# One diffusion step of a two-layer hybrid mixer: first modulation by three operations from PSUM, four early products of x in place of six, and branch parameters set up where the branches begin

## The chip, the cores and the metric

The kernel runs on one core of a Trainium2 chip. The core has five engines that each work through their own list of instructions in order and wait for each other by semaphores: TensorE (PE, matrix products into the accumulation memory PSUM), VectorE (DVE), ScalarE (ACT), GpSimd (POOL) and SyncE (SP, which here only starts transfers from main memory). The metric is the time of one execution on the device in microseconds, as the median of several runs.

## The reference

384 tokens (128 of context, 256 latent) with 2048 channels go through two layers. Each layer modulates its input, multiplies it with one large matrix, runs four branches (an RG-LRU, a neighbourhood attention, a grouped-query attention, an mLSTM), and multiplies their gated outputs with a second matrix:

```python
mod = jax.nn.silu(cond) @ lp['ada_w'] + lp['ada_b']          # 2048 -> 3 * 2048, one row per token kind
shift, scale, gate = jnp.split(mod, 3, axis=-1)
xm = rmsnorm(x, lp['norm_w']) * (1.0 + scale) + shift
pr = split_projection(xm @ lp['w_in'])                       # 2048 -> 7184
...                                                          # branches A to D on slices of pr
y = jnp.concatenate([out_a, out_b, out_c, out_d], axis=-1) @ lp['w_out']
x = x + gate * y
```

Before the first product with `w_in`, then, the norm of x over all 2048 channels and the first values of `shift` and `scale` have to be there. The branches need small per-channel parameters: the RG-LRU the log sigmoid of `lru_lambda` and half of its gate biases, the mLSTM a quarter of its output norm.

## The kernel before

The tokens lie along the free dimension, the channels in 16 chunks (index k) of 128 partitions. Every product in float32 is made of three products of rounded parts: x is split into `xh` and `xl`, each weight tile into `wh` (a rounded copy, made by ACT from the tile `raw` that SP has fetched) and `wl` (the rest, `raw - wh`, made by POOL in pieces of 256 columns). There are three buffers for `raw`. A weight tile covers two chunks k and up to 512 columns.

Layer 0 makes eight passes over the groups of columns `vif`, `ml_q`, `ml_k`, `ml_o`, `lru_gate`, `ml_v`, `lru_x`, `na_q`, `gqa_k`, each pass with two chunks k, because the modulation of all chunks is not known at once. The modulation itself comes in 12 parts s for each layer: part 0 of layer 0 by 16 matmuls of PE (`ada_pe`, two values of k at a time), all others by DVE (`ada_dve`), which multiplies 16 tiles `araw` of the modulation weights (256 KB each, called slices below) with two scalars each and sums in the tile `sbp`, two `SCALAR_TENSOR_TENSOR` to a slice, and then folds the sum (`STREAM_TRANSPOSE`, `TENSOR_REDUCE`, one matmul and the operations on `picked`, in `ada_final`). Part s of layer 0 gives the shift and scale of chunks 2s and 2s + 1.

The list `START` sets the order of the beginning: fetch x and square it, with the matmuls of part 0 between; token `r` makes the inverse norm `rbc` of each token (`rstd_bc`) and multiplies the first chunks of x with it on DVE (`unit_rms`, the early products). The other chunks are multiplied by POOL, in two halves of 128 and 256 tokens, each asked for by `modulate0` of an earlier chunk. `modulate0` makes `xh` on ACT, straight from the multiplied x, and `xmt` and `xl` on DVE. After the last matmul of part 0, ACT copies the row out of PSUM, PE transposes it in four small pieces into a scratch bank, and DVE makes `mod` (the shift) and `Amul` (norm weight times one plus scale) of chunks 0 and 1.

`setup_params` prepares the parameters of the branches: some 20 operations of DVE on tiles of 8 or 16 columns and one exponential on ACT. A helper `defer` runs a function once a counter of the matmul time written so far has passed a number. The scheduler of the framework then decides the final order on each engine, and SP's list holds the fetches of `raw` and of slices in one queue: a fetch of `raw` that waits for its buffer holds back the slices behind it.

Of the kernel before, what the change touches and what calls it, by code (L numbers as in the profile page):

```python
# [16 lines left out]
KC = D // 128  # L17
# [60 lines left out]
def tile_hybrid_step(ctx: ExitStack, tc: tile.TileContext, I, O):  # L78
# [32 lines left out]
    def defer(dt, fn):  # L111
        deferred.append([clock["now"] + dt, fn])
# [33 lines left out]
    def sm(i, n, name):  # L146
        return wrk.tile([128, n], F32, name=name, tag=f"m{i}", bufs=2)

    pers_all = consts.tile([128, T + 384 + PP_W + DEPTH * 128 + 264], F32, name="pers")
    used = [0]  # L150

    def pers(n):
# [13 lines left out]
    def P(n, l=None, parts=2):  # L166
        a, b = PP[n]
        if l is None:
            return prm[:, a:b]
        s = (b - a) // parts  # L170
        return prm[:, a + l * s:a + (l + 1) * s]
# [24 lines left out]
    def stt(out, a, s, b, op0, op1):  # L196
        return nc.vector.scalar_tensor_tensor(out, a, s, b, op0=op0, op1=op1)  # L197
# [32 lines left out]
    def setup_params():  # L230
# [4 lines left out]
        nc.vector.tensor_scalar(hbi, P("bi"), 0.5, None, op0=OP.mult)  # L235
        nc.vector.tensor_scalar(mln, P("mlnorm"), 0.25, None, op0=OP.mult)


    ada_acc = dict(done=0)
    last_ev = {}  # L240

    def order(later, earlier):
        tc.add_manual_dep(later, earlier.name,
                          mybir.DependencyInfo(mybir.DependencyClass.NoSync, mybir.DependencyReason.DATA),
                          reason="issue order")

    def traced(fn):
        bb = nc.cur_bb.bb
        n = len(bb.instructions)
        fn()  # L250
        return bb.instructions[n:]
# [4 lines left out]
                last_ev["v"] = ins  # L256


    def ada_final_mod(l, j0, nj):
        v = mod[:, l, j0:j0 + nj, :]  # L260
        b = P("ada_b", l)[:, j0:j0 + nj]
        nc.vector.tensor_tensor(v, v, b[:, :, None].to_broadcast([128, nj, 2]), op=OP.add)
        if 16 <= j0 < 32:
            nb = P("norm", l)[:, j0 - 16:j0 - 16 + nj]
            stt(Amul[:, l, j0 - 16:j0 - 16 + nj, :], v, 1.0, nb[:, :, None].to_broadcast([128, nj, 2]),
                OP.add, OP.mult)

    sbp = pada.tile([128, 1024], F32, name="sbp")

    def ada_pe(it):  # L270
        t = it["t"]
        raw = it["raw"]
        if t == 0:
            ada_acc["pe"] = accb[3]
        ps = ada_acc["pe"]
        for kk in range(2):
            k = 2 * t + kk
            nc.tensor.matmul(ps[0:2, :], scond[:, k, :], raw[:, kk, :], start=k == 0, stop=k == KC - 1)
        if it["stop"]:
            row = w(0, "adarow")  # L280
            act(row[0:2, :], ps[0:2, :], AF.Copy)
            pt = scr("adat")
            for q in range(4):
                nc.tensor.transpose(pt[:, 2 * q:2 * q + 2], row[0:2, q * 128:(q + 1) * 128], ident[0:2, 0:2])
            for i, j0 in enumerate((0, 16)):
                nc.vector.tensor_copy(mod[:, 0, j0:j0 + 2, :], pt[:, 4 * i:4 * i + 4].rearrange("p (q c) -> p q c", c=2))
                ada_final_mod(0, j0, 2)
            ada_acc["done"] += 1

    quarter = pers(4)  # L290
# [34 lines left out]
    def ada_dve(it):  # L325
        raw = it["raw"]

        def piece(c):
            it["left"] -= 1
            l, s, k = it["l"], it["s"], it["k"]  # L330
            acc = sbp[:, c * 512:(c + 1) * 512]
            sc = scond[:, k, c:c + 1]
            if it["start"]:
                d = nc.vector.tensor_scalar(acc, raw, sc, None, op0=OP.mult)  # L334
            else:
                d = stt(acc, raw, sc, acc, OP.mult, OP.add)
            if "v" in last_ev:
                order(d.ins, last_ev["v"])

        def fold(c):  # L340
            l, s = it["l"], it["s"]
            acc = sbp[:, c * 512:(c + 1) * 512]
            if c == 0:
                ada_acc["red"] = sm(15, 32, "red")
            red = ada_acc["red"]
            turned = wrk.tile([128, 512], F32, name="turned", tag="adasb", bufs=2)
            d = nc.vector.transpose(turned, acc)
            nc.vector.tensor_reduce(red[:, c * 16:(c + 1) * 16], turned.rearrange("p (g i) -> p g i", i=32),
                                    axis=AX.X, op=OP.add)
            if "v" in last_ev:  # L350
                order(d.ins, last_ev["v"])
            if c == 1:
                finals.append((clock["now"] + FLAG, lambda: ada_final(l, s, red)))

        it["left"] = 2
        for c in range(2):
            backlog.append(lambda c=c: piece(c))
        for c in range(2 if it["stop"] else 0):
            backlog.append(lambda c=c: fold(c))
# [95 lines left out]
    def unit_rms(k, eng):  # L455
        for a in (0, TP) if eng is nc.gpsimd else (0,):
            b = T if a or eng is nc.vector else TP
            eng.tensor_tensor(xr[k][:, a:b], xr[k][:, a:b], rbc[:, a:b], op=OP.mult)

    def modulate0(k):  # L460
        x = xr[k]
        t = wrk.tile([128, T], F32, name="xmt", tag="t15", bufs=4)
        for c, (a, b) in enumerate(SEG):
            act(xh[k][:, a:b], x[:, a:b], AF.Identity, bias=mod[:, 0, k, c:c + 1], scale=Amul[:, 0, k, c:c + 1])
        for c, (a, b) in enumerate(SEG):
            nc.vector.tensor_scalar(t[:, a:b], x[:, a:b], Amul[:, 0, k, c:c + 1], mod[:, 0, k, c:c + 1],
                                    op0=OP.mult, op1=OP.add)
        xl[k] = big.tile([128, T], F32R, name=f"xl{k}", tag=f"xl{k}", bufs=1)
        nc.vector.tensor_sub(xl[k], t, xh[k].bitcast(F32))  # L469
        if 6 <= k + 4 < KC:  # L470
            unit_rms(k + 4, nc.gpsimd)

    def split_cat(k):
        act(xh[k], cat[:, k, :], AF.Copy)
# [1074 lines left out]
    for tok in START:  # L1549
        if tok == "x":  # L1550
            for k in xq[0]:
                nc.sync.dma_start(xr[k], I["xT"][:, k, :])
            for k in xq.pop(0):
                square_in(k, xr[k], nc.vector)
        elif tok == "w":
            upto("w", wl, w_dma, pos["w"] + 1)
        elif tok == "r":
            rstd_bc()
            for k in range(6):
                unit_rms(k, nc.vector)  # L1560
        elif tok == "P":
            it = first.pop(0)
            a_dma(it)
            ada_pe(it)
        elif tok == "D":
            it = a_items[pos["a"]]
            upto("a", a_items, a_dma, pos["a"] + 1)
            ada_dve(it)
            it["early"] = True
# [4 lines left out]
    for it in plan:  # L1574
# [6 lines left out]
        elif ty == "mod":  # L1581
            l = it["l"]
            mods.extend((it["req"], l, k) for k in it["ks"] if (l, k) not in ready)
            if it["first"]:
                upto("w", wl, w_dma, cur_w + 4)
                if l == 0:
                    upto("a", a_items, a_dma, n_first + NADA - 1)
                    load_consts()
                for k in it["ks"]:
                    need(l, k)  # L1590
                if l == 0:
                    defer(60.0, setup_params)
        elif ty == "split":
            whole.clear()
            for n4 in range(2):
# [128 lines left out]
```

## Time and profile before

| what | value |
|---|---|
| runs | 1468.54, 1468.83, 1475.76 us, median 1468.83 us |
| the profiled execution | 1480.24 us, of which the span on the core is 1478.4 us |
| PE busy | 1415.2 us, 96% of the span |
| DVE busy | 1080.4 us, 73% |
| POOL busy | 914.5 us, 62% |
| ACT busy | 828.1 us, 56% |

The profiled execution took 11.4 us more than the median run. PE is busy nearly all of the time, so the page's shares say little on where time can be gained: what counts are the stretches in which PE stands still, and what it waits for there. The page's slices show the granted clock of PE at seven tenths of full speed in the first slice of 37 us and at eight tenths in the second.

### The profile page before, as it was taken

The numbers are of one execution on the slowest core, as the hardware profiler recorded it, in microseconds if no ns is written. First come the engines' busy times: TensorE is split into PE (matmuls) and PEld (weight loads), VectorE is DVE, ScalarE is ACT, GpSimd is POOL, SyncE is SP. The second block draws the span as 40 slices with busy tenths as digits, with TensorE's granted clock in tenths as the row PEclk, the third lists the DMA queues.
The fourth block names the chain that finished last, engine by engine and source line by source line (L and its number), as shares of the span: only waits on it lengthen the run. The fifth ranks groups of instructions, "written<-read, shape, count | busy, mean of one in ns | idle before, by whom it ended". The sixth has DMA issues, their size and how long they took to land. (4 is left out here: it accounts for less than half of the span.)

```text
span 1478.4 us, 23865 instructions
## 1 busy us (share of the span) xinstructions
PE 1415.2 (96%) x7999; PEld 1331.2 (90%) x7999; DVE 1080.4 (73%) x2050; ACT 828.1 (56%) x1638; POOL 914.5 (62%) x1242
## 2 busy tenths in 40 slices
PE   6889999899999999999989999999999999899997
PEld 1879999798998799999989999999999789799997
DVE  4889999998899948858568998447667760943533
ACT  4579999765546776553343434234454877363432
POOL 1856666656566765755737666675656774555762
PEclk7899999999999999999999999999999999899999
DMA  8777878686677555565748877654547344355433
GB/s 271 242 231 250 240 230 253 197 253 180 180 209 239 163 165 161 206 222 195 233 130 263 249 243 231 181 159 122 173 142 232 100 128 133 104 175 171 146 122 96
DMA packets 167519, 281.67 MB, mean 191 GB/s; under 512 B 17380, under 2 KB 49380, under 8 KB 167268
## 3 DMA queue, kind: packets, MB, share of 16 engines
q1 hardware_dynamic: 159520, 272.40, 60.4%
q10 hardware_dynamic: 7876, 7.75, 1.6%
q8 instruction: 62, 1.02, 0.3%
q14 instruction: 61, 0.50, 0.1%
HBM read 271.17 MB, written 8.93 MB: 189 GB/s over the span
## 5 line engine op out<-in xcount | busy, mean ns | idle before, releaser
L1284 POOL TENSOR_TENSOR wl<-raw,wh 128x256 fp32r<-128x256 f32 (+1 forms) x1152 | 864.9, 785 | 477.5 <-ACT wh L193 414.3
L1402 PE MATMUL acc<-xh,wh 128*128 128x384 f32 x1630 | 568.1, 349 | 20.0 <-ACT xh L193 10.0
L1402 PE MATMUL acc<-xl,wh 128*128 128x384 f32 x1630 | 554.2, 340 | 0.0
L1402 PE MATMUL acc<-xh,wl 128*128 128x384 f32 x1630 | 552.2, 339 | 0.2 <-POOL wl L1284 0.2
L197 DVE SCALAR_TENSOR_TENSOR sbp<-araw,pers,sbp 128x512 f32<-128x512 f32 x690 | 517.6, 750 | 27.2 <-DMA araw<-in_ada_n 15.6
L193 ACT ACTIVATE wh<-raw 128x1024 fp32r<-128x1024 f32 (+2 forms) x304 | 307.0, 1013 | 324.9 <-PE acc L1402 248.6
L1402 PEld LDWEIGHTS acc<-xh,wh 128*128 128x128 f32 x1630 | 309.0, 190 | 25.7 <-ACT xh L193 10.4
L1402 PEld LDWEIGHTS acc<-xl,wh 128*128 128x128 f32 x1630 | 308.6, 189 | 1.5
L1402 PEld LDWEIGHTS acc<-xh,wl 128*128 128x128 f32 x1630 | 308.1, 189 | 1.2 <-POOL wl L1284 1.1
L1402 PE MATMUL acc<-wh,xl 128*128 128x512 f32 (+2 forms) x452 | 165.4, 366 | 5.4 <-DVE xl L469 2.7
L1402 PE MATMUL acc<-wl,xh 128*128 128x512 f32 (+2 forms) x452 | 163.9, 363 | 0.0
L1402 PE MATMUL acc<-wh,xh 128*128 128x512 f32 (+2 forms) x452 | 163.0, 361 | 0.0
L1402 PEld LDWEIGHTS acc<-wh,xl 128*128 128x128 f32 x452 | 88.5, 196 | 19.3 <-DVE xl L469 4.6
L1402 PEld LDWEIGHTS acc<-wl,xh 128*128 128x128 f32 x452 | 88.0, 195 | 12.5
L1402 PEld LDWEIGHTS acc<-wh,xh 128*128 128x128 f32 x452 | 88.0, 195 | 12.1
L197 DVE SCALAR_TENSOR_TENSOR cat<-acc,pers,xold 128x128 f32<-128x128 f32 (+1 forms) x56 | 20.3, 409 | 66.7 <-PE acc L1402 66.7
L193 ACT ACTIVATE cat<-acc 128x384 f32<-128x384 f32 (+1 forms) x94 | 46.2, 495 | 5.4 <-PE acc L1402 4.8
L193 ACT ACT_TABLE_LOAD x26 | 33.4, 1283 | 10.2 <-DVE arena L891 7.9
L193 ACT ACTIVATE xh<-cat 128x384 fp32r<-128x384 f32 x32 | 16.5, 519 | 40.0 <-PE acc L1402 24.0
L389 DVE TENSOR_TENSOR arena<-arena,sq 128x384 f32<-128x384 f32 x38 | 25.8, 679 | 16.0 <-ACT sq L193 14.5
L1402 PE MATMUL s<-xh,wh 128*128 128x384 f32 x98 | 34.1, 348 | 1.2 <-ACT cat L193 1.2
L334 DVE TENSOR_SCALAR sbp<-araw,pers 128x512 f32<-128x512 f32 x46 | 34.3, 745 | 0.2
(338 smaller groups left out, 1824.0 us busy)
## 6 DMA issues: line engine op xcount, KB each, us to landing
raw<-in_w_in SPq DMA_DIRECT2D x208, 512.0 KB, 4.0
araw<-in_ada_n SPq DMA_DIRECT2D x368, 256.0 KB, 4.3
raw<-in_w_out SPq DMA_DIRECT2D x64, 512.0 KB, 4.0
raw<-in_w_in SPq DMA_DIRECT2D x32, 256.0 KB, 3.0
araw<-in_ada_n SPq DMA_DIRECT2D x8, 512.0 KB, 5.4
xr<-in_xT SPq DMA_DIRECT2D x16, 192.0 KB, 5.7
nac<-in_nac SPq DMA_DIRECT2D x8, 288.0 KB, 4.3
xold<-in_xT SPq DMA_DIRECT2D x3, 768.0 KB, 6.4
```

The costliest lines, as they stand in the source:

```text
L193: return nc.scalar.activation(out, in_, f, bias=bias, scale=scale)
L197: return nc.vector.scalar_tensor_tensor(out, a, s, b, op0=op0, op1=op1)
L334: d = nc.vector.tensor_scalar(acc, raw, sc, None, op0=OP.mult)
L389: eng.tensor_tensor(sqacc, sqacc, s, op=OP.add)
L1284: nc.gpsimd.tensor_tensor(it["lo"][:, kk, cs], raw[:, kk, cs], hv[:, kk, cs], op=OP.subtract)
L1402: last_ev["pe"] = nc.tensor.matmul(out, a, b, start=s0 and i == 0, stop=s1 and i == 2, skip_group_check=not it["first"]).ins
```

## The change

Three edits:

- In the final step of part 0 (`ada_pe`), five operations on DVE (two copies out of PSUM, two additions, one combined operation) become three: one adds the bias to the shift straight from PSUM, one multiplies the scale in PSUM with the norm weight, one adds the tile `nb0` = (1 + bias) * norm weight, which is made once at the start.
- DVE multiplies four chunks of x early instead of six. POOL's products are asked for two chunks ahead instead of four, and begin with chunk 4 instead of chunk 6.
- `setup_params` is deferred to 228 us of the counter instead of 60, and its DVE operations are put behind the last slice product written by then (`last_ev["ada"]`).

```diff
-    pers_all = consts.tile([128, T + 384 + PP_W + DEPTH * 128 + 264], F32, name="pers")
+    pers_all = consts.tile([128, T + 384 + PP_W + DEPTH * 128 + 266], F32, name="pers")
...
+    def late_setup():
+        for ins in traced(setup_params):
+            if ins.engine == mybir.EngineType.DVE:
+                order(ins, last_ev["ada"])
+
...
-    def ada_final_mod(l, j0, nj):
-        v = mod[:, l, j0:j0 + nj, :]
-        b = P("ada_b", l)[:, j0:j0 + nj]
-        nc.vector.tensor_tensor(v, v, b[:, :, None].to_broadcast([128, nj, 2]), op=OP.add)
-        if 16 <= j0 < 32:
-            nb = P("norm", l)[:, j0 - 16:j0 - 16 + nj]
-            stt(Amul[:, l, j0 - 16:j0 - 16 + nj, :], v, 1.0, nb[:, :, None].to_broadcast([128, nj, 2]),
-                OP.add, OP.mult)
+    nb0 = pers(2)
+    stt(nb0, P("ada_b", 0)[:, 16:18], 1.0, P("norm", 0)[:, 0:2], OP.add, OP.mult)
...
-            for i, j0 in enumerate((0, 16)):
-                nc.vector.tensor_copy(mod[:, 0, j0:j0 + 2, :], pt[:, 4 * i:4 * i + 4].rearrange("p (q c) -> p q c", c=2))
-                ada_final_mod(0, j0, 2)
+            pv = pt[:, 0:8].rearrange("p (q c) -> p q c", c=2)
+
+            def per_k(v):
+                return v[:, 0:2][:, :, None].to_broadcast([128, 2, 2])
+
+            nc.vector.tensor_tensor(mod[:, 0, 0:2, :], pv[:, 0:2], per_k(P("ada_b", 0)), op=OP.add)
+            nc.vector.tensor_tensor(Amul[:, 0, 0:2, :], pv[:, 2:4], per_k(P("norm", 0)), op=OP.mult)
+            nc.vector.tensor_tensor(Amul[:, 0, 0:2, :], Amul[:, 0, 0:2, :], per_k(nb0), op=OP.add)
             ada_acc["done"] += 1
...
+            last_ev["ada"] = d.ins
             if "v" in last_ev:
                 order(d.ins, last_ev["v"])
...
-        if 6 <= k + 4 < KC:
-            unit_rms(k + 4, nc.gpsimd)
+        if 4 <= k + 2 < KC:
+            unit_rms(k + 2, nc.gpsimd)
...
             rstd_bc()
-            for k in range(6):
+            for k in range(4):
                 unit_rms(k, nc.vector)
...
                 if l == 0:
-                    defer(60.0, setup_params)
+                    defer(228.0, late_setup)
```

The scheduler moves instructions beyond these edits in about the first third of the program. Later on, the lists of both kernels are the same on every engine, apart from line numbers (up to 5 higher in the changed kernel). Three places matter below.

DVE's list at the first modulation, before: the last two early products (`xr_94`, `xr_95`), the five operations on `pers` (lines 286, 262 and 197), with three slice products between, and the first `xmt`.

```order
L458 TENSOR_TENSOR xr_94<-xr_94,pers 128x384
L458 TENSOR_TENSOR xr_95<-xr_95,pers 128x384
L286 COPY pers<-s_80 128x4 x2
L262 TENSOR_TENSOR pers<-pers 128x4
L197 SCALAR_TENSOR_TENSOR sbp<-araw,pers,sbp 128x512
L262 TENSOR_TENSOR pers<-pers 128x4
L197 SCALAR_TENSOR_TENSOR sbp<-araw,pers,sbp 128x512
L197 SCALAR_TENSOR_TENSOR pers<-pers 128x4
L197 SCALAR_TENSOR_TENSOR sbp<-araw,pers,sbp 128x512
L466 TENSOR_SCALAR xmt<-xr_90,pers 128x128
```

The same place now:

```order
L463 TENSOR_TENSOR xr_93<-xr_93,pers 128x384
L289 TENSOR_TENSOR pers<-s_80,pers 128x4
L290 TENSOR_TENSOR pers<-s_80,pers 128x4
L291 TENSOR_TENSOR pers<-pers 128x4
L197 SCALAR_TENSOR_TENSOR sbp<-araw,pers,sbp 128x512
L471 TENSOR_SCALAR xmt<-xr_90,pers 128x128
```

Two early products are gone, and no slice product stands between the three operations any more.

The lists from 30 to 60 us on the two engines that feed the weights: POOL's list before, from the first `wl` of `ml_q` (four pieces) to those of `ml_k` and the groups behind it (`xr_102` to `xr_105` are chunks 12 to 15).

```order
L1284 TENSOR_TENSOR wl<-raw,wh 128x256 x4
L458 TENSOR_TENSOR xr_102<-xr_102,pers 128x128
L458 TENSOR_TENSOR xr_102<-xr_102,pers 128x256
L458 TENSOR_TENSOR xr_103<-xr_103,pers 128x128
L458 TENSOR_TENSOR xr_103<-xr_103,pers 128x256
L458 TENSOR_TENSOR xr_104<-xr_104,pers 128x128
L458 TENSOR_TENSOR xr_104<-xr_104,pers 128x256
L458 TENSOR_TENSOR xr_105<-xr_105,pers 128x128
L458 TENSOR_TENSOR xr_105<-xr_105,pers 128x256
L1284 TENSOR_TENSOR wl<-raw,wh 128x256 x26
```

Now, the end of the same stretch:

```order
L463 TENSOR_TENSOR xr_103<-xr_103,pers 128x128
L463 TENSOR_TENSOR xr_103<-xr_103,pers 128x256
L463 TENSOR_TENSOR xr_104<-xr_104,pers 128x128
L463 TENSOR_TENSOR xr_104<-xr_104,pers 128x256
L463 TENSOR_TENSOR xr_105<-xr_105,pers 128x128
L1289 TENSOR_TENSOR wl<-raw,wh 128x256 x4
L463 TENSOR_TENSOR xr_105<-xr_105,pers 128x256
L1289 TENSOR_TENSOR wl<-raw,wh 128x256 x22
```

Before the `wl` of `ml_k`, POOL's list held 20 halves of x products; it holds 23 now, and the 24th stands right behind them. SP's list, before, from the fetch of `lru_gate` (the first row) over `ml_v`, `lru_x` and `na_q` to `gqa_k`:

```order
L1271 DMA raw<-in_w_in 128x2x512
L1293 DMA araw<-in_ada_n 128x512
L1271 DMA raw<-in_w_in 128x2x512
L1293 DMA araw<-in_ada_n 128x512 x2
L1271 DMA raw<-in_w_in 128x2x512
L1293 DMA araw<-in_ada_n 128x512 x2
L1271 DMA raw<-in_w_in 128x2x512
L1293 DMA araw<-in_ada_n 128x512 x5
L1271 DMA raw<-in_w_in 128x2x256 x2
```

And now:

```order
L1276 DMA raw<-in_w_in 128x2x512
L1298 DMA araw<-in_ada_n 128x512 x3
L1276 DMA raw<-in_w_in 128x2x512
L1298 DMA araw<-in_ada_n 128x512
L1276 DMA raw<-in_w_in 128x2x512
L1298 DMA araw<-in_ada_n 128x512 x2
L1276 DMA raw<-in_w_in 128x2x512
L1298 DMA araw<-in_ada_n 128x512 x4
L1276 DMA raw<-in_w_in 128x2x256
L1298 DMA araw<-in_ada_n 128x512 x2
```

Seven slices are asked for ahead of the fetch of `ml_v` in both lists. Behind it one slice is now ahead of `lru_x` and three ahead of `na_q`, against two and four, and the last two of part 1 stand behind `gqa_k`.

ACT's list where the mLSTM begins, before (`u` and `arena` are its tiles, `na_q` and `gqa_k` evictions of column groups):

```order
L193 ACTIVATE u<-arena 128x1
L193 ACTIVATE na_q<-acc_112 128x384
L193 ACTIVATE acc_112<-gqa_k 128x256
L193 ACTIVATE arena<-arena,pers 128x256
L193 ACTIVATE arena<-arena 128x128 x4
L193 ACTIVATE na_q<-acc_113 128x384
L193 ACTIVATE arena<-arena 128x128 x3
L193 ACTIVATE na_q<-acc_114 128x384
```

And now:

```order
L193 ACTIVATE u<-arena 128x1
L193 ACTIVATE na_q<-acc_113 128x384
L193 ACTIVATE ls_3566<-ls_3566 128x16
L193 ACTIVATE na_q<-acc_114 128x384
L193 ACTIVATE acc_113<-gqa_k 128x256
L193 ACTIVATE acc_114<-gqa_k 128x256
L193 ACTIVATE na_q<-acc_115 128x384
L193 ACTIVATE arena<-arena,pers 128x256
L193 ACTIVATE arena<-arena 128x128 x7
```

The exponential of `setup_params` (tile `ls`) stands here now, and the mLSTM's own eight operations moved behind all three evictions of `na_q`.

## Rows read from the trace of the kernel before

**Rows 1.** The page: span; busy us (share) of each engine; one group (busy us, mean ns).

```profile
span 1478.4 us, 23865 instructions
...
PE 1415.2 (96%) x7999; PEld 1331.2 (90%) x7999; DVE 1080.4 (73%) x2050; ACT 828.1 (56%) x1638; POOL 914.5 (62%) x1242
...
L193 ACT ACT_TABLE_LOAD x26 | 33.4, 1283 | 10.2 <-DVE arena L891 7.9
```

**Rows 2.** Windows: length; busy us (instructions) of PE, PEld, DVE, ACT, POOL; granted clock, DMA share, GB/s.

```profile
20.00:40.00 20.00, 11.73 (x29) 4.60 (x30) 13.63 (x28) 8.68 (x16) 8.64 (x14) 0.59 0.60 191
40.00:60.00 20.00, 17.24 (x90) 16.09 (x89) 15.92 (x33) 10.56 (x20) 19.91 (x31) 0.85 0.75 232
80.00:100.00 20.00, 14.31 (x73) 13.12 (x73) 15.97 (x31) 12.91 (x30) 9.26 (x14) 0.83 0.70 217
120.00:160.00 40.00, 40.00 (x244) 38.70 (x243) 37.41 (x64) 38.34 (x83) 29.86 (x42) 1.00 0.78 231
```

**Rows 3.** Timeline of PE: start us, length us, instructions; idle before, and its releaser.

```profile
39.38 0.69 PE L1402 MATMUL acc<-xh,wh 128*128 128x384 f32 x1 [5.77 <-ACT xh L193]
...
50.71 0.34 PE L1402 MATMUL s<-xh,wl 128*128 128x384 f32 x1
...
85.61 0.69 PE L1402 MATMUL acc<-xh,wh 128*128 128x384 f32 x1 [4.27 <-ACT xh L193]
...
282.48 0.69 PE L1402 MATMUL acc<-xh,wh 128*128 128x384 f32 x1 [1.50 <-DVE lru_x L1371]
...
344.31 0.61 PE L791 MATMUL s<-mlc,arena 128*128 128x129 f32 x4
...
496.19 0.69 PE L865 MATMUL s<-xcs,lwh 128*128 128x388 f32 x2 [3.39 <-DVE picked L305]
```

**Rows 4.** Timeline of DVE, same columns.

```profile
31.31 4.43 DVE L458 TENSOR_TENSOR xr<-xr,pers 128x384 f32<-128x384 f32 x6 [0.57 <-ACT pers L193]
...
35.67 0.22 DVE L286 COPY pers<-s 128x4 f32<-128x4 f32 x2
...
55.61 0.75 DVE L197 SCALAR_TENSOR_TENSOR sbp<-araw,pers,sbp 128x512 f32<-128x512 f32 x1 [4.08 <-DMA araw<-in_ada_n]
...
66.05 6.30 DVE L197 SCALAR_TENSOR_TENSOR sbp<-araw,pers,sbp 128x512 f32<-128x512 f32 x8
...
72.38 1.31 DVE L347 STREAM_TRANSPOSE turned<-sbp 128x512 f32<-128x512 f32 x2
...
81.75 0.18 DVE L305 TENSOR_TENSOR picked<-s,pers 128x32 f32<-128x32 f32 x1
...
342.30 0.28 DVE L762 TENSOR_TENSOR arena<-arena,s 128x128 f32<-128x128 f32 x1
```

**Rows 5.** Timeline of ACT, same columns.

```profile
33.44 1.60 ACT L193 ACTIVATE wh<-raw 128x544 fp32r<-128x544 f32 x2 [0.28 <-DMA raw<-in_w_in]
...
38.34 1.86 ACT L193 ACTIVATE xh<-xr,pers 128x128 fp32r<-128x128 f32 x4 [1.17 <-DVE pers L197]
...
333.94 0.49 ACT L193 ACTIVATE arena<-arena,pers 128x256 f32<-128x256 f32 x1
...
336.97 0.47 ACT L193 ACTIVATE na_q<-acc 128x384 f32<-128x384 f32 x1
```

**Rows 6.** POOL, 30 to 63 us: groups (busy us, mean ns | idle before), then its timeline.

```profile
L458 POOL TENSOR_TENSOR xr<-xr,pers 128x256 f32<-128x256 f32 x10 | 7.4, 737 | 0.0
L458 POOL TENSOR_TENSOR xr<-xr,pers 128x128 f32<-128x128 f32 x10 | 5.4, 544 | 30.2 <-ACT pers L193 30.2
...
47.92 14.13 POOL L1284 TENSOR_TENSOR wl<-raw,wh 128x256 fp32r<-128x256 f32 x20
```

**Rows 7.** Timeline of SP's queue: start us, us of issuing, DMAs issued.

```profile
29.31 1.83 SPq L1271 DMA_DIRECT2D raw<-in_w_in  x3
...
51.26 0.89 SPq L1293 DMA_DIRECT2D araw<-in_ada_n  x2
```

**Rows 8.** A group of DVE instructions, 28 to 75 us: busy us, mean ns.

```profile
L262 DVE TENSOR_TENSOR pers<-pers 128x4 f32<-128x4 f32 x2 | 0.8, 395 | 0.0
```

## The prediction

> **What bounds the kernel now.** I read the page first: PE is busy 96% of a span of 1478.4 us [rows 1], so only stretches in which PE waits can give time back. The windows show where these are. From 20 to 40 us PE has next to no product of the layer to do, from 80 to 100 us it is busy 14.31 of 20 us at a granted clock of 0.83, and from 120 to 160 us it is full at clock 1.00 [rows 2]. PE's timeline names the waits: the first product of the layer starts at 39.38 after 5.77 us of idling for `xh`, the second pass starts at 85.61 after 4.27 us for the next `xh`, the eighth at 282.48 waiting for DVE, and the RG-LRU costs 3.39 us at 496.19, where DVE has not yet read `picked` [rows 3]. The change can act on the first of these directly, on the second through DVE and POOL, and on the others through the new order.
>
> **The start.** DVE's six early products begin at 31.31, and the copies out of PSUM stand behind them at 35.67: 0.727 us each [rows 4]. ACT's first `xh` follows at 38.34, and waited for DVE's `pers` [rows 5]. With four products the three new operations start at 31.31 + 4 x 0.727 = 34.22. For the two that read PSUM I take the 0.22 us of both copies [rows 4], for the third, which reads two tiles of SBUF and waits for the one before it, the 0.395 us of the line 262 additions [rows 8]; done at 34.84. If all three cost 0.395 it is 35.40, if all cost 0.18, as `picked` out of PSUM [rows 4], 34.76. ACT is the next limit: its conversions of the first two weight tiles began at 33.44 when the transfer landed and took 1.60 us, to 35.04 [rows 5]. The `ml_q` tile among them is fetched at 29.31 in both lists [rows 7], so I put `xh` at 35.04: **3.3 us earlier**, with bounds 2.9 and 3.6. The slice products that stood between no longer do, and DVE's first `xl` comes earlier by as much.
>
> SBUF is where this could fail: POOL works on x all that time. The line 262 additions with both inputs in SBUF took 0.395 us beside it; the read of PSUM at 81.75, with POOL idle, took 0.18 [rows 4, 8]. The Trainium skill, "SBUF — State Buffer", section "Who interferes with whom", says that a DVE instruction with two SBUF inputs and a POOL instruction that reads SBUF exclude each other, while one with at most one SBUF input, outside the modes that use both ports, does not contend. By that rule only the third operation can be held, by at most one POOL product, and the start would come at the late bound instead of the early one; the rows agree as far as they go.
>
> **POOL's four halves.** POOL is busy 19.91 of 20 us from 40 to 60 [rows 2], without a gap in its list, so what is added pushes all behind it. Two chunks more are 2 x (0.737 + 0.544) = 2.56 us [rows 6]; I take that, and for a lower bound 2.0 us, in case POOL runs freer when DVE has two products less. Of the four halves three (0.737 + 2 x 0.544 = 1.83 us) now stand ahead of the `wl` of `ml_k`, whose 20-piece run started at 47.92 with 0.707 us a piece [rows 6]. It would start at 49.75; its first piece is done at 50.45, its third at 51.87. PE used the first at 50.71 [rows 3] and, three products further, the third at about 51.2 (a product takes 0.164 us at full clock: 40.00 us for 244 [rows 2]). PE 3.3 us earlier wants them at 47.4 and stands still; at the third piece it is 0.7 us later than before (0.3 with the lower bound). So the lead of the start is **lost again by 52 us (+3.3)**. I count it as nothing left, because the rest of the pass had slack: PE needs 24 products of 0.164 us, 3.9 us, for a tile that POOL makes in 4 x 0.707 = 2.8 us.
>
> **The second pass.** It needs part 1 of the modulation, 16 slices on DVE. DVE stood 4.08 us for a slice until 55.61, then ran to the fold at 72.38 without a pause, over the 18 products of 9 slices (the first and the last eight are shown [rows 4]). The last eight took 0.79 us each (66.05 to 72.38), so 18 are 14.2 us of the 16.77; the rest, 2.55 us, is what `setup_params` cost there, and it leaves. What holds the slices is SP's queue: the pair at 51.26 went out right behind the fetch of `ml_v` [rows 7], which waits until POOL has freed the buffer of `ml_k` (47.92 + 4 x 0.707 = 50.75). With POOL later the fetches move by 1.83 us for `ml_v` and 2.56 for those behind, and now one slice passes there instead of two. With 4.35 us from issue to landing (51.26 to 55.61) slice 8 lands at 57.4, slices 9 and 10 at 61.0, the next four from 63.7, the last two at about 66.6. DVE at 1.58 us a slice ends at about 73.6, **1.2 us later** in spite of the 2.55 us; with POOL at its lower bound 0.6 later, with nothing late 2.55 earlier. Behind the fold four slice products instead of seven stand ahead of `picked` (in both lists a fixed number, at 81.75 before [rows 4]): 3 x 0.79 = **2.4 us earlier**. Together the second pass starts 1.2 us earlier, at 84.4, with bounds 4.9 and 0.6 earlier. What the passes behind it do is unchanged, PE is full from 120 us on, and the wait at 282.48 moves along.
>
> **The branches.** `setup_params` goes to where the mLSTM begins: some 20 short DVE operations there, in place of slice products that would have stood between the mLSTM's own steps, and one exponential on ACT. DVE's last step before PE's products with `mlc` ended at 342.58 and PE came at 344.31 without waiting [rows 3, 4]: 1.7 us of slack cover it. I take **nothing**, and what it costs without that cover is a rival below. In the RG-LRU the matmul at 496.19 waits for `picked`, which stood on DVE behind two products that take their input from ACT (one for each direction of a block) and now stands behind one; I take half of the 3.39 us, **-1.5** (bounds -3.39 and +2.6, two more table loads of 1.283 us that ACT's new list has there [rows 1, 3]). The one operation for `nb0` falls in DVE's idling at the start, and costs nothing; on the path it would be below 0.4 us.
>
> **Sum.** -3.3 + 3.3 - 1.2 + 0 - 1.5 = -2.7 us. The profiled execution of 1480.24 us would become 1477.5; against the median of 1468.83, 11.4 us lower, I give 1466.1 us. A measurement of this kernel tells about 0.5%, 7.3 us, from no change.
>
> **The rivals.**
>
> *Nothing gained.* POOL's halves cost their full 2.56 us ahead of everything, the slices land later still, and the second pass starts when it did; the RG-LRU's wait stays. For it speaks that POOL has no gap for 30 us and that SP queues slices behind it; against it that 2.55 us of DVE work are gone. 1468.8 us, within 1.
>
> *The stall goes as a whole.* If the slices arrive as before, DVE saves 2.55 + 2.4 = 4.9 us and the second `xh` comes at 80.7. PE's wait of 4.27 us nearly goes, and with it the fall of the clock to about half that follows such waits (0.83 over the window [rows 2]): some 1.6 us more. With the RG-LRU's 3.39 us it makes -10, 1458.8 us. Against it speaks the arithmetic of POOL above.
>
> *Slower, by the mLSTM.* On ACT the mLSTM's eight steps, which began at 333.94, now stand behind the third eviction of `na_q`, which ended at 337.44 [rows 5]: 3.5 us later. On DVE 20 short operations stand among its steps, at 0.18 to 0.395 us 3.6 to 7.9 us, against some four displaced slice products (3.2 us). If the two add up, the chain is 3.5 + 4.7 = 8.2 us later, of which 1.7 us of slack are covered: PE waits 6.5 us at line 791 (the wait decides as soon as it passes 1.7 us), and the clock falls behind it as after 85.61, 1.6 us. Less the 1.2 us of the second pass that is +6.9, 1475.7 us; with ACT's part alone +0.6.
>
> By the same page of the Trainium skill, the section named above, short DVE operations on two SBUF tiles are held only while POOL reads SBUF, so the same 20 operations would be cheaper at the branches than among POOL's run at 40 to 60 us; by that rule the slower rival stays near its low end. No row of before shows them there.
>
> **How the numbers follow.** Forecast 0.46; nothing gained 0.22; the stall gone 0.17; slower 0.10; 0.05 for other effects of the moved order, either way. The forecast's own range is -5 to -1, 1464 to 1468. Leaving out the far half of the second and third rivals, 1458 to 1474 holds a little over 8 in 10. Faster by over 0.5% (below 1461.5) come most of the third case and little else: 0.16. Slower by over 0.5% (above 1476.2): the far half of the slower case and some of the rest, 0.08. Between: 0.76.
>
> **What would show it.** DVE's `pers` operations should end near 34.9 and PE's first product of the layer start near 36.1; else the early products did not hold it. PE should then wait 2 to 4 us for `wl` at about 47 us, where it did not before; if not, the POOL step is wrong, and the start is kept. DVE should wait for slices several times between 52 and 67 us and reach the fold between 71 and 74; the second pass should start near 84.4. The mLSTM's products at line 796 of the new kernel should start without a wait. The prediction is wrong if PE's lead at 60 us is over 2 us, or if a new wait of over 3 us stands at a branch.

## Result, and the profile after

The changed kernel takes 1490.08 us (median of 5, 1482.90 to 1492.38). The kernel before, timed beside it, took 1468.83 us (1466.91 to 1476.00). The ratio is 1.0109, 95% interval [1.0076, 1.0142]: about 16 us **slower**. The forecast was 1466.1 us, no change, with a range of 1458 to 1474. The two medians lie further apart than the ratio says, because the executions of each program fall into two groups, 1467 to 1469 and 1476 us before, 1483 and 1490 to 1492 us after (about 15 us apart, group against group), most likely by a wait of 0.9 or 7.0 us for `gth` late in the run (last section); both profiled executions, 1480.24 us before and 1491.37 us after, have the long wait, so their traces can be compared.

The page after: span; busy us and share of each engine; ACT's table loads.

```profile
span 1489.6 us, 23863 instructions
...
PE 1413.6 (95%) x7999; PEld 1330.3 (89%) x7999; DVE 1085.0 (73%) x2047; ACT 830.5 (56%) x1640; POOL 919.8 (62%) x1246
...
L193 ACT ACT_TABLE_LOAD x28 | 35.9, 1283 | 10.7 <-DVE arena L896 8.1
```

PE does the same work in a span that is 11.2 us longer, and ACT loads two tables more than in [rows 1]. The windows say where the time goes (columns as in [rows 2]):

```profile
80.00:100.00 20.00, 15.72 (x76) 14.47 (x76) 16.61 (x31) 13.22 (x30) 9.81 (x15) 0.83 0.73 244
...
360.00:380.00 20.00, 15.79 (x81) 14.36 (x79) 14.67 (x29) 7.87 (x21) 11.78 (x15) 0.83 0.44 135
...
500.00:520.00 20.00, 15.80 (x62) 12.44 (x62) 19.93 (x31) 12.99 (x20) 17.49 (x21) 0.91 0.52 148
520.00:540.00 20.00, 18.13 (x81) 15.76 (x81) 14.20 (x21) 16.79 (x26) 17.40 (x24) 0.91 0.43 135
```

The window at 80 us is little better than before. The other three lie in the two branches, where PE was full at clock 1.00 in the kernel before:

```profile
360.00:380.00 20.00, 19.98 (x125) 18.69 (x124) 18.88 (x44) 8.87 (x23) 12.92 (x18) 1.00 0.59 177
500.00:520.00 20.00, 20.00 (x92) 16.78 (x91) 19.86 (x33) 19.44 (x31) 15.62 (x20) 1.00 0.47 134
520.00:540.00 20.00, 20.00 (x117) 19.52 (x116) 13.12 (x27) 13.81 (x27) 14.22 (x21) 1.00 0.52 146
```

PE's timeline after names the waits:

```profile
35.89 0.69 PE L1407 MATMUL acc<-xh,wh 128*128 128x384 f32 x1 [2.97 <-ACT xh L193]
...
50.52 0.44 PE L1407 MATMUL s<-xh,wl 128*128 128x384 f32 x1 [3.81 <-POOL wl L1289]
...
85.36 0.44 PE L1407 MATMUL acc<-xh,wh 128*128 128x384 f32 x1 [2.85 <-ACT xh L193]
...
350.17 0.71 PE L796 MATMUL s<-mlc,arena 128*128 128x129 f32 x4 [2.02 <-DVE arena L766]
...
367.07 0.48 PE L818 MATMUL s<-pers,arena 128*128 128x128 f32 x1 [4.21 <-ACT arena L193]
...
505.41 0.45 PE L870 MATMUL s<-xcs,lwh 128*128 128x388 f32 x1 [2.69 <-POOL xcs L855]
...
514.22 0.63 PE L870 MATMUL s<-xcs,lwh 128*128 128x388 f32 x2 [1.28 <-ACT arena L193]
...
529.45 0.75 PE L870 MATMUL s<-xcs,lwh 128*128 128x388 f32 x2 [1.87 <-ACT arena L193]
```

The start is earlier as forecast, then PE waits for `wl` as forecast. At the mLSTM two waits are new (L796 and L818 are lines 791 and 813 of the kernel before): PE came to line 791 without waiting [rows 3], and to line 813 as well:

```profile
360.44 0.27 PE L813 MATMUL s<-pers,arena 128*128 128x128 f32 x1
```

In the RG-LRU three waits stand in place of the one for `picked` [rows 3]. To size them, the start of the same product of PE's main loop is compared in the two traces: the 240th stood at 95.03 us before, the 1440th (ahead of the mLSTM) at 313.56, the 2080th (ahead of the RG-LRU) at 465.87, the 2400th (behind it) at 552.09. After, these are 0.67, 2.84, 10.27 and 15.06 us later. So the mLSTM lost 7.4 us and the RG-LRU 4.8; 3.9 us came back between there and the end, in several places that were not traced further. In the mLSTM's stretch PE idles 9.0 us in place of 3.5 (a wait of 2.28 us for `arena`, at 351.95 before, is gone) and is busy 1.9 us longer for the same products; in the RG-LRU's it idles 6.1 us in place of 3.4 and is busy 2.1 us longer.

DVE after, at the start, at the second pass and in the mLSTM:

```profile
30.86 3.36 DVE L463 TENSOR_TENSOR xr<-xr,pers 128x384 f32<-128x384 f32 x4 [0.38 <-ACT pers L193]
...
34.39 0.43 DVE L291 TENSOR_TENSOR pers<-pers 128x4 f32<-128x4 f32 x1
...
73.89 1.31 DVE L352 STREAM_TRANSPOSE turned<-sbp 128x512 f32<-128x512 f32 x2
...
80.89 0.18 DVE L309 TENSOR_TENSOR picked<-s,pers 128x32 f32<-128x32 f32 x1
...
82.48 1.08 DVE L316 TENSOR_TENSOR pers<-picked,pers 128x4 f32<-128x4 f32 x2
...
336.78 0.16 DVE L234 TENSOR_SCALAR pers<-pers 128x16 f32<-128x16 f32 x1
336.85 0.72 DVE L235 TENSOR_SCALAR pers<-pers 128x16 f32<-128x16 f32 x1
...
350.04 0.27 DVE L767 TENSOR_TENSOR arena<-arena,s 128x128 f32<-128x128 f32 x1
...
362.46 0.73 DVE L809 TENSOR_SCALAR ss<-ss 128x3 f32<-128x3 f32 x1
```

All 20 parameter operations lie between 336.25 and 349.2, together 6.2 us (14 of them take 0.15 to 0.22 us each, 6 take 0.43 to 0.73). The last step ahead of the products with `mlc` ends at 350.31, where it ended at 342.58 [rows 4].

### The profile page after: what moved, and what is told of

Same layout as the page of the kernel before. It is cut to its first block, busy times and chain, and to the rows that moved or that the text cites. A ratio compares the mean times of both kernels' runs of the same rounds, so it can differ in the third digit from the quotient of the medians.

```text
span 1489.6 us, 23863 instructions
## 1 busy us (share of the span) xinstructions
PE 1413.6 (95%) x7999; PEld 1330.3 (89%) x7999; DVE 1085.0 (73%) x2047; ACT 830.5 (56%) x1640; POOL 919.8 (62%) x1246
## 5 line engine op out<-in xcount | busy, mean ns | idle before, releaser
L1407 PE MATMUL s<-xh,wl 128*128 128x384 f32 x98 | 33.7, 347 | 5.3 <-POOL wl L1289 5.3
```

What stands on the lines that cost most here:

```text
L1407: last_ev["pe"] = nc.tensor.matmul(out, a, b, start=s0 and i == 0, stop=s1 and i == 2, skip_group_check=not it["first"]).ins
```

## The experiments

Theory A: the loss comes from the 20 parameter operations among the mLSTM's steps, and from the RG-LRU's new order that comes with them. (The expectations name this order by ACT's list. The lists of POOL, DVE and PE differ there too, and they change together in every kernel, so what follows holds for the order as a whole.) Theory B: it comes from POOL's four halves at the start. Theory C: any edit changes the scheduler's order somewhere, and this one happened to be bad. The other rivals are named where they were put up. In every kernel the placement of the parameters is one number, the plan time in `defer`.

**The three edits apart (e1 to e4).** e1 takes only the hunks of `ada_final_mod` and of the part behind the transposes, e2 only `range(4)` and `k + 2`, e3 only the late parameters. e4 is the changed kernel with

```diff
-                    defer(228.0, late_setup)
+                    defer(60.0, setup_params)
```

> Only the first modulation by three operations from PSUM; six early products and the parameters at 60 us as before. Theory A (the loss comes from the parameter operations among the mLSTM's steps): none of them moves, so no new wait at the mLSTM or the RG-LRU; the first product of the layer comes 1 to 2 us earlier (the six products still stand ahead of the operations, 2 x 0.727 us later than in the change), 1465 to 1469 us. Theory B (the loss comes from the early part: POOL's four halves and what follows): no halves are added, so 1464 to 1468. Theory C (any edit reshuffles the scheduler's order at the branches and this loses): 1472 or more, with a wait of over 3 us at the RG-LRU's products.

> Only four early products in place of six, POOL the two more chunks; the copies and the modulation as before, parameters at 60 us. Theory A: the copies out of PSUM start 1.45 us earlier, POOL's four halves take that back by 52 us, and nothing changes at the branches: 1467 to 1471. Theory B: it keeps most of the loss, 1476 or more, with PE already 3 us later than before at 180 us. Theory C: 1472 or more, lost behind 300 us.

> Only the branch parameters set up at the branches; six early products and the modulation as before. Theory A: the mLSTM's step ahead of the products with mlc is 6 to 8 us later, PE waits about 2 us there and about 4 us some 15 us later; with the RG-LRU 8 to 14 us lost, the second pass gives 2 to 4 back: 1474 to 1481. Theory B: 1464 to 1469, since DVE saves 2.55 us ahead of the second pass and nothing is added early. Theory C: 1472 or more, but not more than the other two edits alone.

> The whole change but for the parameters, which are set up at 60 us as before. Theory A: the waits at the mLSTM and the RG-LRU that the change brought are gone, 1465 to 1471. Theory B: the loss stays, 1482 to 1490. Theory C: 1472 to 1490, with waits of over 3 us at other places of the branches.

Measured: e1 1.0023 [1.0006, 1.0041], e2 1.0000 [0.9990, 1.0011], e3 1.0077 [1.0053, 1.0101], e4 1.0042 [1.0019, 1.0066]. The parameters alone bring most of the loss, 11 of 16 us, and they bring it at the two branches (table below). B and C fall: e1, e2 and e4 lose nothing there. In time theory A missed two of them: e1 is 3 us over before, where it had none, and e4 is 6 us over before, 4 above the top of its range; of these 6 us 2.7 are there ahead of the mLSTM.

**Where the operations stand (e5 to e8).** The changed kernel (e5, e6) and the kernel before with late parameters alone (e7, e8), at 130, 250, 215 and 220 us of plan time:

```diff
-                    defer(228.0, late_setup)
+                    defer(130.0, late_setup)
```

> The whole change, but the parameter operations 98 us earlier, between slice products of the passes; every engine's order in the mLSTM and the RG-LRU is that of before. Theory A (two losses, the operations among the mLSTM's steps, 5 to 8 us, and the RG-LRU's new order on ACT, 4 to 5 us): both are gone, 1471 to 1475, what the run with the parameters at 60 us gave. Theory D (POOL's halves and the new start weaken the lead, so that a branch loses wherever the operations stand): still 1478 or more.

> The whole change, but the parameter operations behind the first block of the mLSTM; that block's order is that of before on DVE, ACT and POOL, while the RG-LRU keeps the order of the change (one block at a time on ACT, two table loads more). Theory A: no new wait at the first block of the mLSTM, but the RG-LRU still loses 4 to 5 us: 1475 to 1480. Rival E (the RG-LRU only hands on the lateness of the mLSTM): 1471 to 1475, as with the operations 98 us earlier.

> The parameters alone, 13 us ahead of where the change puts them: among the slice products and the forget gate's operations, ahead of the mLSTM's first step; the RG-LRU's order is that of before. Theory A: what the deferral gains at the second pass (2.8 us) stays, 1465 to 1468. Rival F (20 operations more anywhere near the branches cost 5 us or more): 1472 or more.

> The same, 5 us later: the operations stand in nearly the same rows on DVE, still ahead of the mLSTM's first step, but the RG-LRU has the order of the change on ACT, with two table loads more. Theory A: 4 to 5 us over the run with the parameters 13 us ahead, 1469 to 1473. Rival E: within 1.5 us of that run.

Measured: e5 1.0026 [1.0004, 1.0047], e6 1.0052 [1.0030, 1.0074], e7 1.0032 [1.0009, 1.0054], e8 1.0068 [1.0044, 1.0091]. D falls by e5: with the new start and POOL's halves, but the operations elsewhere, 12 of the 16 us are gone. E falls by e6 and e8: the mLSTM of e6 loses nothing, and its RG-LRU still loses 3.6 us. PE in the RG-LRU of e8, the order of the change:

```profile
495.98 0.45 PE L872 MATMUL s<-xcs,lwh 128*128 128x388 f32 x1 [2.08 <-POOL xcs L857]
...
504.77 0.62 PE L872 MATMUL s<-xcs,lwh 128*128 128x388 f32 x2 [1.31 <-ACT arena L193]
...
519.78 0.62 PE L872 MATMUL s<-xcs,lwh 128*128 128x388 f32 x2 [1.65 <-ACT arena L193]
```

and of e7, the order of before:

```profile
498.67 0.62 PE L872 MATMUL s<-xcs,lwh 128*128 128x388 f32 x2 [1.71 <-DVE picked L311]
...
518.22 0.62 PE L872 MATMUL s<-xcs,lwh 128*128 128x388 f32 x2 [1.03 <-ACT arena L193]
```

ACT in the same stretch, 460 to 560 us, its table loads in e7 and then in e8:

```profile
L193 ACT ACT_TABLE_LOAD x7 | 9.0, 1283 | 2.3 <-DVE arena L898 1.6 <-DVE arena L901 0.5
```

```profile
L193 ACT ACT_TABLE_LOAD x9 | 11.5, 1283 | 2.6 <-DVE arena L898 2.5
```

The same three releasers stand in the changed kernel. For e7 and e8 theory A was wrong in one point: standing ahead of the mLSTM's first step did not make the operations free, the mLSTM lost 3.0 and 4.5 us. Rival F had the time of e7 right; e6, whose mLSTM loses nothing, speaks against its "anywhere near the branches".

**The second wait, and the operations without the start (e9 to e12).** e9 is the changed kernel again. e10 orders POOL:

```diff
+            last_ev.setdefault("ss", pw.ins)
...
+                order(lp.ins, last_ev["ss"])
```

e11 is late parameters alone at 130; e12 is the kernel before with a second `setup_params` into spare tiles by `defer(228.0, late_spare)`.

> The changed kernel itself, timed beside the next three. All theories: 1482 to 1492, 12 to 16 us over the kernel before where both or neither pay the late wait for gth (a wait of PE near the end that was 7.0 us in some executions and 0.9 in others, of before and of variants alike).

> The changed kernel with two of POOL's subtractions (xcs, the RG-LRU's first convolution) put behind the mLSTM's ss instead of ahead of it; nothing else moves. Theory A, with POOL's order as the cause of the second wait: PE's wait of 4.2 us after the mLSTM's first block falls to about 1.3 us, the clock of that stretch does not fall, 3 to 6 us faster than the changed kernel. Rival G (ss is late because DVE reaches it late, behind the parameter operations): less than 1.5 us faster, the wait stays above 3 us.

> The parameters alone, at 130 us of the plan: between slice products while PE is full. Theory A: second pass 2.4 to 2.9 us earlier and kept, orders of the mLSTM and RG-LRU as before, 1466 to 1468 (or 2 to 3 us under before, state for state). Rival F (the operations cost as much wherever they stand): 1469 to 1471, no gain.

> The kernel before, parameters set up at 60 us as there, and once more among the mLSTM's steps into tiles that nobody reads (work added, nothing left out). The RG-LRU has the new order. Theory A: nothing is gained at the start; a wait of 1 to 3 us at the products with mlc, and 4 to 5 us in the RG-LRU: 5 to 9 us over before. Rival E: 1 to 4 us over before. Theory D (the loss needs the new start): within 2 us of before at the mLSTM.

Measured: e9 1.0102 [1.0071, 1.0133], e10 1.0098 [1.0064, 1.0132], e11 1.0010 [0.9987, 1.0033], e12 1.0078 [1.0049, 1.0107]. e12 is the plainest test: nothing but the operations is added, and the mLSTM loses 7.9 us, the RG-LRU 3.4; with 11 us over before it costs more than the 5 to 9 of theory A, and D and E fall once more. e11 did not gain the 2 to 3 us that theory A had: its time, 1.5 us over before (between 1.9 under and 4.8 over), fits rival F as well. Its trace has PE 2.2 us earlier at 95 us, 0.8 earlier at 314, and no loss at the branches. e10 was undecided in time: 0.6 us under e9, with a wait that stays above 3 us, as rival G had it. PE and POOL of e10:

```profile
367.47 0.33 PE L819 MATMUL s<-pers,arena 128*128 128x128 f32 x1 [3.12 <-ACT arena L193]
```

```profile
362.18 3.48 POOL L1291 TENSOR_TENSOR wl<-raw,wh 128x256 fp32r<-128x256 f32 x4 [2.58 <-ACT wh L193]
365.62 1.36 POOL L810 TENSOR_TENSOR ss<-ss,pers 128x3 f32<-128x3 f32 x1
```

POOL of the changed kernel:

```profile
360.69 3.47 POOL L1289 TENSOR_TENSOR wl<-raw,wh 128x256 fp32r<-128x256 f32 x4 [2.58 <-ACT wh L193]
364.12 1.65 POOL L855 TENSOR_TENSOR xcs<-xc,xcs 128x256 fp32r<-128x256 f32 x2
365.73 0.85 POOL L810 TENSOR_TENSOR ss<-ss,pers 128x3 f32<-128x3 f32 x1
```

DVE and POOL of the kernel before:

```profile
358.39 0.15 DVE L804 TENSOR_SCALAR ss<-ss 128x3 f32<-128x3 f32 x1
```

```profile
358.62 1.16 POOL L805 TENSOR_TENSOR ss<-ss,pers 128x3 f32<-128x3 f32 x1 [2.15 <-DVE ss L804]
```

DVE's step of `ss` starts at 358.39 before, at 362.46 after and at 363.96 in e10. With `xcs` out of the way POOL's step starts 1.7 us behind it in place of 3.3, still held by a run of `wl` (0.23 us behind it before), and PE waits 3.12 us in place of 4.21. So the two `xcs` explain 1.1 us, and rival G only half of what is left: PE comes to the products 0.4 us behind the start of DVE's step in e10, 2.05 behind it before, so 1.7 us are DVE's lateness, and 1.4 us lie between the starts of DVE's step and of POOL's. POOL's list tells the same in other runs: ahead of the first `ss` it holds 276 pieces of `wl` in the kernel before and in all seven kernels whose mLSTM loses nothing, 280 to 288 in all ten executions whose mLSTM loses 2.0 us or more (table below). No run moves `ss` back ahead of these pieces and nothing else.

**How many operations (e13 to e16).** e13 is the changed kernel with 227 in place of 228. e14 and e15 split `setup_params`: the log-sigmoid at 130 or 215, the five scalings at 228. e16 is four products and late parameters at 130, with the copies of before.

```diff
+                    defer(130.0, lambda: late_setup(setup_params))
+                    defer(228.0, lambda: late_setup(setup_rest))
```

> The whole change, the parameter operations asked for 1 us of plan time earlier: all 20 now stand ahead of the mLSTM's first step, and the RG-LRU has the order of before on ACT. Theory A (20 operations among the mLSTM's steps, and the RG-LRU's order that comes with them): no RG-LRU loss and about half of the mLSTM's, as the parameters alone had it 13 us ahead; 3 to 7 us over before and 6 to 10 under the changed kernel. Rival H (the operations cost the same on either side of the mLSTM's first step): 10 us or more over before.

> The whole change, the log-sigmoid (15 operations and the exponential) at 130 us of the plan, only the 5 scalings left among the mLSTM's steps; RG-LRU in the order of before. Theory A by count: a quarter of the DVE delay, no wait at the products with mlc, the mLSTM 1 to 4 us later by its end, 3 to 6 us over before. Rival I (any operation there reorders the steps): mLSTM 7 us or more, 9 us over before.

> As the run with five late, but the log-sigmoid at 215 us of the plan, just ahead of the mLSTM; the RG-LRU has the order of the change. Theory A: what the run with five late gives, and 3 to 6 us more, of which 3 to 5 fall between the RG-LRU's start and end. If the RG-LRU's order costs nothing by itself: within 2 us of the run with five late.

> Four early products and the parameters at 130 us of the plan, modulation by the copies as before; orders at the branches as before. If the gains at the start and at the second pass add up: 2 to 4 us under before. If POOL's halves take them back, as the changed kernel's first pass shows: within 2 us of before.

Measured: e13 1.0044 [1.0032, 1.0056], e14 1.0056 [1.0037, 1.0075], e15 1.0084 [1.0066, 1.0102], e16 1.0013 [1.0005, 1.0022]. One microsecond of plan time, from 228 to 227, gives more than half of the loss back. H falls. e14 is 8 us over before, 2 more than theory A had, but in its trace 5.2 us are there ahead of the mLSTM, which itself loses 2.0: I falls too. DVE, POOL and PE of e14 at the second wait:

```profile
362.84 0.71 DVE L811 TENSOR_SCALAR ss<-ss 128x3 f32<-128x3 f32 x1
```

```profile
365.14 0.85 POOL L812 TENSOR_TENSOR ss<-ss,pers 128x3 f32<-128x3 f32 x1
```

```profile
366.48 0.33 PE L820 MATMUL s<-pers,arena 128*128 128x128 f32 x1 [3.48 <-ACT arena L193]
```

PE waits for `ss` here without having waited at the products with `mlc`. e15 ends 4 us above e14; its RG-LRU is 5.5 us longer than that of e14, its mLSTM 1.2. In e15 all 20 operations came to stand ahead of the mLSTM, the five scalings too, so it differs from e14 in more than the order of the RG-LRU. e16 gains nothing, and no run was faster than before.

All runs, us by which each stretch is longer than in the profiled execution of before, worked out from the four products named above. Between them stand, for the first block of the mLSTM, PE's wait at the products with `mlc` (wait 1), the time by which POOL's step of `ss` starts behind DVE's, and PE's wait for what follows from it (wait 2):

```
       operations among the  wait 1  POOL    wait 2  mLSTM   RG-LRU's   RG-LRU
       first mLSTM steps             behind                  order
before 0                     0       0.23    0               before
after  20                    2.02    3.27    4.21    +7.4    new        +4.8
e9     20                    2.00    3.28    4.21    +9.4    new        +4.7
e3     20                    1.47    3.26    4.23    +7.5    new        +3.4
e10    20                    2.01    1.66    3.12    +6.7    new        +3.6
e12    20                    1.06    2.49    3.74    +7.9    new        +3.4
e15    0, 20 just ahead      0       2.48    3.77    +3.1    new        +4.7
e8     0, 20 just ahead      0.12    2.47    2.48    +4.5    new        +2.7
e6     0, 20 behind          0       0.23    1.31    +0.3    new        +3.6
e7     0, 20 just ahead      0.43    2.40    3.52    +3.0    as before  -1.5
e13    0, 20 just ahead      0.13    2.10    2.00    +3.8    as before  -1.0
e14    5                     0       2.30    3.48    +2.0    as before  -0.8
e5     0                     0       0.24    1.24    -0.6    as before  -0.7
e11    0                     0       0.24    0       -0.3    as before   0.0
e16    0                     0       0.23    0       -0.3    as before  +0.9
e4     0                     0       0.24    0       +0.1    as before  -0.7
e1     0                     0       0.24    1.25    -1.2    as before  -0.7
e2     0                     0       0.24    1.24    -0.7    as before  -0.5
```

The rows "after" and "e9" show how far one program repeats itself: the changed kernel lost 7.4 us at the mLSTM in one execution and 9.4 in the other, with the same waits.

## Why the prediction was wrong

**The start** was right: DVE's third operation ended at 34.82 (forecast 34.84), the first product of the layer came at 35.89 (36.1). That DVE's figure is met to 0.02 us is luck: its four products began 0.45 us earlier than before and took 3.3 us in place of 2.9. ACT, which the prediction made the limit with 35.04, was not one: its conversions were done at 34.30, and its `xh` waited for DVE until 34.85. One reading was wrong too: POOL was not idle at the read of PSUM at 81.75, so the 0.18 us of that read were taken beside a busy POOL.

```profile
78.17 5.54 POOL L1284 TENSOR_TENSOR wl<-raw,wh 128x256 fp32r<-128x256 f32 x8 [1.35 <-ACT wh L193]
```

How much of the 3.5 us is the change is not certain: in e12, whose start is that of before, this product came 1.6 us earlier than in the trace of before, in e7 0.5 us later.

**POOL's four halves** were right: the `wl` of `ml_k` started at 49.74 (49.75), PE waited 3.81 us at 50.52 and 0.58 at 51.90 (2 to 4 forecast), and the lead was gone. The term was a little small: PE was not level with before but 1.2 us behind it where that kernel stood at 73 us. e2 shows it alone: 2.0 us earlier at the first product, 0.35 us later at 73 us.

**The second pass** was mis-sized: forecast 1.2 us earlier, measured 0.25 (85.36). The fold was at 73.89 (73.6) and `picked` at 80.89, 0.9 us earlier. Then the two `pers` operations took 1.08 us where they took 0.46 before:

```profile
83.34 0.46 DVE L312 TENSOR_TENSOR pers<-picked,pers 128x4 f32<-128x4 f32 x2
```

Both of them lay beside a run of eight `wl` products of POOL now (79.37 to 84.91); before, that run (78.17 to 83.71) ended just as the second of them began. PE was 0.7 us late at 95 us and 2.8 at 314; of the 2.2 us between only 0.8 were traced, at the eighth pass (PE waits 1.99 us for `red` against 1.21).

**The branches** were the step that failed: "1.7 us of slack cover it. I take **nothing**". DVE's step came 7.7 us later and PE 3.8 us later, so DVE fell back by 3.9 us against PE; less the slack of 1.7 that leaves 2.2 us, and PE waited 2.02. The rival that was called *slower, by the mLSTM* had the place and nearly the size, 6.5 us of waiting with 1.6 of clock against a loss of 7.4, but the size by luck: it put all the waiting at line 791, and of its parts ACT's did not come, since ACT's chain did not wait for `na_q` (its step waited 0.2 us for DVE). What it lacked was a second wait: DVE's step of `ss` came late for PE too (1.7 us later against PE than before), and in POOL's new list a weight tile more and two `xcs` stood ahead of POOL's step, which started 3.27 us behind DVE's in place of 0.23. PE waited 4.21 us at L818 with the clock at 0.83 in that window. The price was put together from the first wait only, and the whole rival got 0.10. The prediction's own sign of being wrong, a new wait of over 3 us at a branch, is this second wait.

**The RG-LRU** was entered as -1.5 with an upper bound of +2.6, two table loads. Measured: +4.8. The 3.39 us for `picked` did go, as hoped, but the order that removed it finishes the two directions of the first block one after the other on ACT (hence the two table loads) and has other lists on POOL and DVE, and PE waited 2.69 us for POOL's `xcs` and 1.28 and 1.87 us for ACT's `arena`: 5.84 us, 2.4 more than before, with the clock at 0.91 in two windows where it was 0.92 in one. The bound priced the loads and left out what the rest of the order makes PE wait for; which of the lists does it, no run tells apart. In eight executions with this order the RG-LRU is 2.7 to 4.8 us longer, in nine with the order of before -1.5 to +0.9.

What stays open: how much of the mLSTM's loss POOL's list makes by itself. Where the operations stand just ahead of the mLSTM it loses 3.0 to 4.5 us with hardly a first wait (0.43 us at most) and a second one of 2.0 to 3.8 us, so what the table shows there points at POOL's list and not at DVE's delay; e13 has a wait of 3.48 us for DVE's `na_q` besides. Open too is why three operations and four products together (e4) are 6 us slower when each alone is 0 to 3.

## What to carry to other kernels

Work that is moved off a busy start is not hidden by the share of free time where it lands, but by the slack of each step of the chain that it lands in: 20 operations, some 6 us on DVE, cost nothing measurable at 130 us of plan time, among sums that nobody waits for, and 11 us among the mLSTM's steps with the order that came with them. Follow the chain past the first late step: what is handed on to another engine there has to queue again, and the list of that engine may have changed with the edit. And where a scheduler orders the program, look for the loop whose order flips, and price the waits of the new order, not only the instructions that it adds.

## What the runs showed that was not expected

The same program runs in one of two ways through a stretch near 1275 us (the products of `cat` and `gqa_k` with `gqk`), and the time differs by some 6 to 8 us. The changed kernel was profiled twice. PE's wait for `gth` (us in total, times, longest), from the list of waits of the first profile (1491.37 us) and of e9 (1485.86 us):

```profile
PE acc L1407 <- DVE gth L197: 7.0, 1, 7.0
```

```profile
PE acc L1407 <- DVE gth L197: 0.9, 1, 0.9
```

DVE and POOL in the first:

```profile
1273.63 2.58 DVE L197 SCALAR_TENSOR_TENSOR cat<-cat,arena,gqk 128x128 f32<-128x128 f32 x4
```

```profile
1273.74 3.08 POOL L1289 TENSOR_TENSOR wl<-raw,wh 128x256 fp32r<-128x256 f32 x4 [2.46 <-ACT wh L193]
```

and in e9:

```profile
1275.47 1.13 DVE L197 SCALAR_TENSOR_TENSOR cat<-cat,arena,gqk 128x128 f32<-128x128 f32 x4
```

```profile
1275.57 8.36 POOL L1289 TENSOR_TENSOR wl<-raw,wh 128x256 fp32r<-128x256 f32 x1 [2.46 <-ACT wh L193]
```

POOL starts 0.10 to 0.11 us behind DVE in both. In the first DVE's four operations take 2.58 us in place of 1.13 and POOL runs at 0.77 us a piece. In e9 DVE runs undisturbed, and POOL's first piece alone takes 8.36 us, in which DVE works through some 25 operations; the pieces behind it take 0.73 to 1.3 us each. All 18 profiled executions of this study have the one or the other: 7.0 us for `gth` and no piece above 1.2 us there in eight, 0.9 us for `gth` and one piece of 8.3 to 8.4 us in ten. The ratios of the experiments mix executions of both kinds; the stretches of the table end ahead of this place. The Trainium skill, "SBUF — State Buffer", section "Who interferes with whom", says that a DVE instruction with two SBUF inputs and a POOL instruction that reads SBUF exclude each other, and that issue order decides who blocks; the rows agree that either can be the one that waits. What decides it here they do not show, since DVE's first operation starts first in both.
